# A diffusion-transformer step in fp32 on one core: where the second layer's modulation dots stand, and where three buffers of token sums lie

## The chip, the cores and the metric

The kernel runs on one core of one Trainium2 chip. A core has a matrix engine (TensorE, PE in the profile, its weight loads as PEld), a vector engine (VectorE, DVE), a scalar engine (ScalarE, ACT), GpSimd (POOL), a queue engine that issues transfers (SyncE, SP), and 16 DMA engines between main memory and the on-chip SBUF; matrix products land in PSUM. The metric is the device time of one execution in microseconds, the median of several runs.

## The reference, cut to what matters

Two layers act on 512 tokens of width 1024: 256 image tokens ("latent") and 256 context tokens. Each layer is a half feed-forward, a mixer (attention in layer 0, an mLSTM in layer 1), and a second half feed-forward. All of them are modulated by a vector per token group.

```python
def modulate(h, shift, scale):
    return h * (1.0 + scale) + shift

def half_ffn(h, shift, scale, gate, w_in, w_out, g, b):
    xm = modulate(h, shift, scale)
    a, u = jnp.split(xm @ w_in, 2, axis=-1)
    y = (jax.nn.silu(a) * u) @ w_out
    return post_norm(h, 0.5 * gate * y, g, b)
```

The hidden width is 2816, 22 blocks of 128. Shift, scale and gate are nine vectors of 1024 per layer, and each comes from the product of `silu(c)` with a 1024 x 9216 matrix `ada_w`, once for the latent tokens' vector `c` and once for the context tokens' vector. For layer 1 only the first feed-forward and the mixer's inputs need the context tokens' part, so the later chapters need one vector alone. Everything is fp32.

## The kernel before

**Products.** An fp32 product is made of three products in a reduced format: every operand is split into a high and a low part, and `mm3` issues high x high, high x low and low x high into the same PSUM tile (L234, by far the largest group of TensorE). Splitting (`split`) is a cast on ScalarE (L218) and a subtraction on VectorE (L223). Weights come as 512 KB tiles of 128 x 1024 over the SP queue (L203, a ring of three raw tiles), are split into a ring of seven pairs, and then feed TensorE.

**Feed-forwards.** Four run in this order with the mixers between: layer 0 first half, attention, layer 0 second half (here "block one", about 520 to 965 us), layer 1 first half ("block two", about 915 to 1330 us), mLSTM, and the last. In blocks one and two `ffn` does each feed-forward in two halves of 11 hidden blocks. In the first half, 11 units of 48 matmuls 512 wide make the hidden activations: `ffn_g` takes a silu on ScalarE (L558), a gate multiply on VectorE (L559) and a split. Four units form a "lead" whose calls for side work come together at the lead's end; each further unit j has one call behind it and two pieces of a residual (`residual`, VectorE at L533). Then eight output products of 33 matmuls 512 wide, one for each block of 128 output features, are added into the running state by VectorE (L679). In the second half the 11 units are done by `fast_in`: it computes the two-by-two block product of weights and tokens with seven instead of eight block products (a Strassen–Winograd scheme), 84 matmuls 256 wide in a unit. The products are issued in the order a11, a12, s1, s2, a22, s4, s3. Four of them (a11, a12, s1, s4) read the tokens as they are. s2, a22 and s3 read sums and differences of token blocks that are prepared once, by `fast_sums`: additions at L578, L582, L585, L587 and L590, each followed by a split. That preparation stands behind the fifth and sixth output product of the first half (d = 4 and 5, `SUMSAT = 4`). The second half then ends with its own output products: four 512 wide, and four in two halves 256 wide.

**The token sums' buffers.** `fast_operands` opens two buffers, `th` and `tl`, for the high and the low parts of three sums of 4 x 256 columns. They lie behind other buffers at bytes 196576 and 208864 of each partition, both 224 bytes past a multiple of 256, and so do all three sums within them. The tokens as they are lie at multiples of 256; the stationary weights lie 64 bytes past one.

**Modulation dots.** A tile of 128 outputs x 1024 inputs of `ada_w` is loaded by `ada_load` (L321, ring of two tiles named "ada", SP queue), and `ada_dot` (L327) multiplies it on VectorE with a vector that all partitions hold, with the sum accumulated: one instruction gives 128 outputs of one vector. The dots are pinned, that is, they keep their place in program order on VectorE. Layer 1 has 72 tiles; the first 40 get two dots (both vectors, a "pair"), the last 32 one dot (a "single"): 112 dots. `silu_c`, `silu_load` and `silu` make the vectors: two broadcast loads of 512 KB and two silu on ScalarE (L296). The buffers share room with those of `fast_in`, and so are closed and opened again. `emit` spreads the dots with hooks that `ffn` calls: behind each unit of the first half as many tiles as make four dots (`DOTS[0]`), behind each output product of the first half three (`DOTS[1]`), until the block's own list is empty. Block one's list has 28 pairs: 22 behind the units, six behind the first three output products. Block two's list has 12 pairs and 32 singles: the pairs and 20 singles behind the units, 12 singles behind the first four output products.

Of the kernel before, what the change touches and what calls it, by code (L numbers as in the profile page):

```python
# [86 lines left out]


SUMSAT = 4
DOTS = (4, 3)  # L90

TAILSTEP = {(0, 3, 1): 'bmccccccc', (1, 0, 2): 'c', (1, 0, 6): 'v', (1, 1, 7): 'rxxxxxxxx'}
MTAILSTEP = {(0, 7, 0): 'bmccccccc', (1, 0, 3): 'c', (1, 1, 0): 'v', (1, 6, 0): 'r', (1, 7, 2): 'xxxxxxxx'}
# [72 lines left out]
class Body:  # L166
# [123 lines left out]
    def silu_load(self, pin=lambda ins: ins):  # L290
        for v in range(2):
            pin(self.nc.sync.dma_start(self.cb[:, v, :], self.a["c2"][v : v + 1, :].broadcast_to([P, D])))

    def silu(self, pin=lambda ins: ins):
        for v in range(2):
# [265 lines left out]

    def fast_operands(self, st):

        self.th, self.tl = (self.t([P, 3, ND // 2, TL], F32R, pool=st) for _ in range(2))

    def fast_sums(self, i):

        V = self.nc.vector
        lo, up = slice(2 * i, 2 * i + 2), slice(ND // 2 + 2 * i, ND // 2 + 2 * i + 2)
        made = lambda k: (self.th[:, k, lo, :], self.tl[:, k, lo, :])  # L570

        def at(ks, g):
            return self.xh[:, ks, g[0] : g[1]], self.xl[:, ks, g[0] : g[1]]

        def whole(ks, g):
            o = self.tmp().rearrange("p (k f) -> p k f", k=2)
            h, l = at(ks, g)
            V.tensor_tensor(out=o, in0=h.bitcast(F32), in1=l.bitcast(F32), op=ALU.add)  # L578
# [12 lines left out]
        self.split(d, *made(2))  # L591

    def fast_in(self, j, w_in, st):

        nc, V, S = self.nc, self.nc.vector, self.nc.scalar
        half = 4 * P
        r0, r1 = (self.raw(w_in[2 * j + i]) for i in range(2))
        sums = self.t([P, 4 * half], tag="sums", bufs=1, pool=st)
        part = lambda x, i: x[:, i * half : (i + 1) * half]
        a11, a21, a12, a22 = part(r0, 0), part(r0, 1), part(r1, 0), part(r1, 1)  # L600
        s1, s2, s4, s3 = (part(sums, i) for i in range(4))
        add = lambda o, x, y: V.tensor_tensor(out=o, in0=x, in1=y, op=ALU.add)  # L602
# [12 lines left out]
        of = lambda k0, g: lambda k: self.x(k0 + k, g)  # L615
        made = lambda i: lambda k: (self.th[:, i, k, :], self.tl[:, i, k, :])

        def product(o, name, x, first, last):
            for k in range(ND // 2):
                c = slice(k * P, (k + 1) * P)  # L620
                self.mm3(o, [y[:, c] for y in w[name]], x(k), first and k == 0, last and k == ND // 2 - 1, group=False)

        x, yv, z = self.mm()[:, :TL], self.mm(), self.mm()[:, :TL]
        y, v = yv[:, :TL], yv[:, TL:]
        a, u = self.tmp(), self.tmp()
        product(x, "a11", of(0, LAT), True, False)
# [12 lines left out]
        u2 = u.rearrange("p (n f) -> p n f", n=2)  # L639
        V.scalar_tensor_tensor(u2, x[:, None, :].broadcast_to([P, 2, TL]), -1.0, u2, ALU.mult, ALU.subtract)  # L640
        V.tensor_tensor(out=a, in0=a, in1=u, op=ALU.mult)
        gh, gl = self.gt[j] = tuple(self.t([P, self.gw], F32R, tag=k, bufs=self.gn, pool=self.gp) for k in ("gh", "gl"))
        self.split(a, gh, gl)

    def ffn(self, layer, s, gate, groups, side, start=None, cpool=None):
# [4 lines left out]
        with self.tc.tile_pool(name=f"ffn{li}", bufs=1) as gp:  # L650
# [34 lines left out]
            for hf in range(2):  # L685
# [35 lines left out]
                body = ND - TAIL if hf else ND  # L721
                if fast:
                    more.close()
                for d in range(body):
                    if cpool and not hf and d == SUMSAT:
                        cpool.close()
                        self.n += 1
                        more = ExitStack()
                        st = more.enter_context(self.tc.tile_pool(name=f"st{self.n}", bufs=1, side="right"))
                        self.fast_operands(st)  # L730
                    unit_out(hf, d, w, allg)
                    if cpool and not hf and d >= SUMSAT and d - SUMSAT < 2:
                        self.fast_sums(d - SUMSAT)
                    call("out", hf, d)
                if body < ND:
                    w = Keep(self, w.chunks, SH, w)
                    self.fine = True
                    for g in groups:
                        for d in range(body, ND):
                            unit_out(hf, d, w, g, TAILSTEP)  # L740
                    self.steps('B')


    def ffn_last(self, layer, gate):
# [820 lines left out]
def emit(ctx, tc, a, out):  # L1565
    b = Body(ctx, tc, a, out)
    nc, V, S = b.nc, b.nc.vector, b.nc.scalar
    b.setup()
    b.setup_rest()
    cpool = b.silu_c()  # L1570
    both2 = (0, 1)
    queue = [
        [(0, p, both2) for p in range(16, 72)],
        [(1, p, both2) for p in range(28)],
        [(1, p, both2) for p in range(28, 40)] + [(1, p, (0,)) for p in range(40, 72)],
    ]
# [9 lines left out]
    def side(key, coef, keep=(True, True), nxt=True, ada=(), alone=False, fast=False):  # L1586
        def pop():
            for _ in range(3 if len(ada) > 40 else 2):
                if ada:
                    b.ada(*ada.pop(0))  # L1590

        def dots(n):
            while n > 0 and ada:
                n -= len(ada[0][2])
                b.ada(*ada.pop(0))

        get = once(key, coef)

        b.begin = lambda g: b.norm(g, get, keep[0 if g == LAT else 1], nxt, alone)
        s = {}  # L1600
        for j in range(NF):
            s["in", j] = (lambda: dots(DOTS[0])) if fast else pop
        for d in range(ND):
            s["out", 0, d] = (lambda: dots(DOTS[1])) if fast else pop
        return s

    both = (LAT, CTX)
    b.ffn(0, 0, once("g0", lambda: b.half_gate(0, 2)), both, side("n0", lambda: b.ln_mod(0, 0, (0, 3)), ada=queue[0]), start)
    assert not queue[0]
    cpool.close()  # L1610
    b.attention(lambda: b.shift_(0, 5), side("n1", lambda: b.ln_mod(0, 1, (0, 6))))
    cpool = b.silu_c()
    b.silu_load()
    b.silu()
    b.ffn(0, 1, once("g1", lambda: b.half_gate(0, 8)), both, side("n2", lambda: b.ln_mod(0, 2, (1, 0)), ada=queue[1], fast=True), cpool=cpool)
    assert not queue[1]
    cpool = b.silu_c()
    b.silu_load()
    b.silu()
    b.ffn(1, 0, once("g2", lambda: b.half_gate(1, 2)), both, side("n3", lambda: b.ln_mod(1, 0, (1, 3)), (True, False), ada=queue[2], fast=True), cpool=cpool)  # L1620
    assert not queue[2]
# [95 lines left out]
```

## Time and profile before

| | |
|---|---|
| runs | 1657.2, 1662.06, 1662.81 us (median 1662.06) |
| profiled execution | 1661.01 us, its span 1659.1 us |
| mean granted clock of TensorE | 0.992 |
| TensorE's matmuls busy | 1624.8 us, 98% of the span |
| VectorE busy | 1354.8 us, 82% |
| ScalarE busy | 743.6 us, 45% |

The span runs from the first to the last instruction that the profiler saw; the rest of the profiled execution's own time, 1.9 us, lies around it. Busy times are sums over an engine's instructions, and matmuls are pipelined, so a busy TensorE is not one at its peak. "PEclk", the granted clock, is the share of full speed that the throttle allowed. "Idle before" is the time an engine stood still ahead of an instruction, put down to the event that released it last. A time such as 1059.67 is counted from the span's start.

### The profile page before, as it was taken

The page shows a single profiled execution, that of the slowest core. Times are in us where ns is not written, and L with a number is a line of the kernel's source. Part 1 is how long each engine was busy: PE and PEld are TensorE (multiplying, and loading weights), DVE is VectorE, ACT ScalarE, POOL GpSimd, SP SyncE. Part 2 cuts the span into 40 slices and gives each one's busy share as a digit, 9 for nine tenths or more (in the row PEclk, how much of TensorE's full clock was granted, in tenths as well). Part 3 has the DMA queues.
Part 4 walks back from the last instruction along what each step waited for, and adds up shares of the span by engine and source line. Part 5 has one row for each costly group of instructions (what it writes and reads, how often), then busy time and mean ns, then how long its engine had stood idle before and what let it go on. Part 6 is the DMA issues. An engine that isn't in the chain of part 4 may idle for free. (4 is left out here: it accounts for less than half of the span.)

```text
span 1659.1 us, 26570 instructions
## 1 busy us (share of the span) xinstructions
PE 1624.8 (98%) x10308; PEld 1463.5 (88%) x10308; DVE 1354.8 (82%) x2689; ACT 743.6 (45%) x1267; POOL 62.3 (4%) x76
## 2 busy tenths in 40 slices
PE   9999999999989999999999999899999999999998
PEld 6888888899978998889999988689999989999987
DVE  5899977749898979999965888779975967897687
ACT  5532132314765443325652424215651566656542
POOL 0000000001010200000000100000000100020000
PEclk9999999999999999999999999898999999999999
DMA  9577766622203157733352267743351342438552
GB/s 372 188 234 234 246 203 193 200 64 84 64 1 113 54 158 223 218 113 117 113 179 69 84 203 251 256 126 103 127 153 55 111 134 78 128 115 253 179 178 89
DMA packets 72207, 251.54 MB, mean 152 GB/s; under 512 B 7952, under 2 KB 10768, under 8 KB 72080
## 3 DMA queue, kind: packets, MB, share of 16 engines
q1 hardware_dynamic: 71504, 249.05, 47.3%
q8 instruction: 81, 1.33, 0.3%
q10 hardware_dynamic: 576, 0.79, 0.1%
q14 instruction: 46, 0.38, 0.1%
HBM read 248.76 MB, written 1.05 MB: 151 GB/s over the span
## 5 line engine op out<-in xcount | busy, mean ns | idle before, releaser
L234 PE MATMUL t<-t,t 128*128 128x256 f32 (+2 forms) x8412 | 1332.6, 320 | 19.3 <-ACT t L218 15.1
L234 PEld LDWEIGHTS t<-t,t 128*128 128x128 f32 x8412 | 1199.4, 189 | 140.1 <-ACT t L218 17.6
L218 ACT CAST t<-t 128x1024 fp32r<-128x1024 f32 (+3 forms) x521 | 428.4, 843 | 481.7 <-PE t L234 233.4
L223 DVE TENSOR_TENSOR t<-t,t 128x256 fp32r<-128x256 f32 (+2 forms) x740 | 513.6, 728 | 116.9 <-ACT t L218 113.2
L327 DVE SCALAR_TENSOR_TENSOR t<-t,t 128x1024 bf16<-128x1024 f32 x224 | 263.8, 1221 | 28.2 <-DMA t<-in_ada_w 27.3
L894 PE MATMUL t<-t,t 128*128 128x256 f32 (+1 forms) x256 | 79.4, 310 | 0.0
L896 PE MATMUL t<-t,t 128*128 128x256 f32 (+1 forms) x256 | 78.7, 307 | 0.0
L895 PE MATMUL t<-t,t 128*128 128x256 f32 (+1 forms) x256 | 78.4, 306 | 0.0
L558 ACT ACTIVATE t<-t 128x512 f32<-128x512 f32 (+1 forms) x71 | 34.3, 488 | 95.4 <-PE t L234 95.3
L679 DVE SCALAR_TENSOR_TENSOR t<-t,t,t 128x256 f32<-128x256 f32 x96 | 42.6, 478 | 41.6 <-PE t L234 41.6
L559 DVE TENSOR_TENSOR t<-t,t 128x512 f32<-128x512 f32 (+1 forms) x71 | 38.9, 552 | 34.4 <-PE t L234 28.0
L454 POOL TENSOR_TENSOR t<-t,t 128x256 f32<-128x256 f32 x30 | 23.5, 785 | 1142.2 <-ACT t L444 1140.9
L1409 PE MATMUL t<-t,t 128*128 128x512 f32 (+3 forms) x286 | 60.2, 366 | 1.9 <-ACT t L1486 1.0
L822 PE MATMUL t<-t,t 128*128 128x512 f32 (+1 forms) x300 | 60.5, 364 | 0.0
L1409 PEld LDWEIGHTS t<-t,t 128*128 128x128 f32 (+2 forms) x286 | 43.8, 159 | 18.3 <-issue 2.3
L822 PEld LDWEIGHTS t<-t,t 128*128 128x128 f32 x300 | 51.5, 189 | 8.9
L444 ACT ACTIVATE t<-t 128x256 f32<-128x256 f32 x72 | 26.1, 411 | 72.0 <-DVE t L437 72.0
L534 ACT ACTIVATE t<-t,t 128x256 f32<-128x256 f32 x64 | 29.4, 503 | 56.6 <-DVE t L533 56.5
L894 PEld LDWEIGHTS t<-t,t 128*128 128x128 f32 x256 | 48.3, 189 | 2.6
L895 PEld LDWEIGHTS t<-t,t 128*128 128x128 f32 x256 | 48.2, 188 | 2.6
L896 PEld LDWEIGHTS t<-t,t 128*128 128x128 f32 x256 | 48.1, 188 | 2.5
L602 DVE TENSOR_TENSOR t<-t,t 128x512 f32<-128x512 f32 x66 | 45.3, 686 | 0.6
(200 smaller groups left out, 1066.3 us busy)
## 6 DMA issues: line engine op xcount, KB each, us to landing
t<-in_ffn_in SPq DMA_DIRECT2D x168, 512.0 KB, 4.0
t<-in_ada_w SPq DMA_DIRECT2D x137, 512.0 KB, 4.3
t<-in_ffn_out SPq DMA_DIRECT2D x66, 512.0 KB, 4.3
t<-in_ffn_last SPq DMA_DIRECT2D x22, 512.0 KB, 3.6
t<-in_att_in SPq DMA_DIRECT2D x12, 512.0 KB, 3.5
t<-in_att_out SPq DMA_DIRECT2D x8, 512.0 KB, 3.5
t<-in_ml_qk SPq DMA_DIRECT2D x8, 512.0 KB, 3.6
t<-in_ml_v SPq DMA_DIRECT2D x8, 512.0 KB, 3.6
```

The source lines that it names most:

```text
L218: self.behind(self.nc.scalar.copy(h, x))
L223: self.behind(self.nc.vector.tensor_tensor(out=ls, in0=xs, in1=hs.bitcast(F32), op=ALU.subtract))
L234: mm = lambda *k, **kw: self.nc.tensor.matmul(*k, skip_group_check=not group, **kw)
L327: ins = nc.vector.scalar_tensor_tensor(self.tmp().bitcast(BF16), r, 1.0, self.cb[:, v, :], ALU.mult, ALU.mult, accum_out=to)
L559: V.tensor_tensor(out=sl, in0=sl, in1=pu[:, :n], op=ALU.mult)
L602: add = lambda o, x, y: V.tensor_tensor(out=o, in0=x, in1=y, op=ALU.add)
L679: V.scalar_tensor_tensor(z, y[:, gg[0] - t0 : gg[1] - t0], gate()[:, v, d : d + 1], z, ALU.mult, ALU.add)
L822: pin(nc.tensor.matmul(o, gs[g], ws[k][w][:, i : i + n], start=k == k0 and g == w == 0, stop=k == k1 - 1 and g == 1,))
L894: mm(o, self.xh[:, k, c], wh, start=k == 0, stop=False)
L895: mm(o, self.xh[:, k, c], wl, start=False, stop=False)
L896: mm(o, self.xl[:, k, c], wh, start=False, stop=k == ND - 1)
L1409: mm = lambda *k, **kw: pin(nc.tensor.matmul(*k, **kw))
```

## The change

Three things are changed; all arithmetic stays.

1. The second layer's dots are one list, `later`, and each block takes its own numbers from it: block one four dots behind each unit, two pairs behind each of the first four output products of the first half, and one pair behind each of the four 512-wide output products of the second half (68 dots); block two three behind each unit (rounded up to whole pairs: six pairs, then 24 singles) and two singles behind each of the first four output products (44 dots). Its entry for the second half finds the list empty.
2. For the dots in the second half's output products the two vectors are loaded and their silu is taken there, inside `ffn` (`silu_all`), and the open buffers are handed to the next feed-forward. Block two does so too, and its vectors are not read again.
3. The three sums' high and low parts lie in one buffer, at byte 196352, a multiple of 256. Sum 0 and sum 1 (read by s2 and s3) follow one another at multiples of 256; sum 2 (read by a22) lies `FLIP` = 56 floats, that is 224 bytes, past one.

```diff
 SUMSAT = 4
-DOTS = (4, 3)
+FLIP = 56
+DOTS = {
+    1: {("in",): 4, ("out", 0): 3, ("out", 1): 2},
+    2: {("in",): 3, ("out", 0): 2, ("out", 1): 3},
+}
...
+    def silu_all(self):
+        pool = self.silu_c()
+        self.silu_load()
+        self.silu()
+        return pool
...
     def fast_operands(self, st):
 
-        self.th, self.tl = (self.t([P, 3, ND // 2, TL], F32R, pool=st) for _ in range(2))
+        n = ND // 2 * TL
+        x = self.t([P, 6 * n + FLIP], F32R, pool=st)
+        at = [2 * i * n + (FLIP if i == 2 else 0) for i in range(3)]
+        self.made = [[x[:, a + p * n : a + (p + 1) * n].rearrange("p (k f) -> p k f", f=TL) for p in range(2)] for a in at]
...
-        made = lambda k: (self.th[:, k, lo, :], self.tl[:, k, lo, :])
+        made = lambda k: [x[:, lo, :] for x in self.made[k]]
...
-        made = lambda i: lambda k: (self.th[:, i, k, :], self.tl[:, i, k, :])
+        made = lambda i: lambda k: [x[:, k, :] for x in self.made[i]]
...
                 if fast:
                     more.close()
+                    cpool = self.silu_all()
                 for d in range(body):
...
                     self.steps('B')
+        return cpool
...
-    queue = [
-        [(0, p, both2) for p in range(16, 72)],
-        [(1, p, both2) for p in range(28)],
-        [(1, p, both2) for p in range(28, 40)] + [(1, p, (0,)) for p in range(40, 72)],
-    ]
+    queue = [(0, p, both2) for p in range(16, 72)]
+    later = [(1, p, both2) for p in range(40)] + [(1, p, (0,)) for p in range(40, 72)]
...
-        def dots(n):
-            while n > 0 and ada:
-                n -= len(ada[0][2])
-                b.ada(*ada.pop(0))
+        def some(n):
+            while n > 0 and later:
+                n -= len(later[0][2])
+                b.ada(*later.pop(0))
...
         for j in range(NF):
-            s["in", j] = (lambda: dots(DOTS[0])) if fast else pop
+            s["in", j] = (lambda: some(dots["in",])) if dots else pop
         for d in range(ND):
-            s["out", 0, d] = (lambda: dots(DOTS[1])) if fast else pop
+            s["out", 0, d] = (lambda d=d: some(dots["out", 0] if d < SUMSAT else 0)) if dots else pop
+            s["out", 1, d] = lambda: some(dots.get(("out", 1), 0))
...
-    cpool = b.silu_c()
-    b.silu_load()
-    b.silu()
-    b.ffn(0, 1, once("g1", lambda: b.half_gate(0, 8)), both, side("n2", lambda: b.ln_mod(0, 2, (1, 0)), ada=queue[1], fast=True), cpool=cpool)
-    assert not queue[1]
-    cpool = b.silu_c()
-    b.silu_load()
-    b.silu()
-    b.ffn(1, 0, once("g2", lambda: b.half_gate(1, 2)), both, side("n3", lambda: b.ln_mod(1, 0, (1, 3)), (True, False), ada=queue[2], fast=True), cpool=cpool)
-    assert not queue[2]
+    cpool = b.silu_all()
+    cpool = b.ffn(0, 1, once("g1", lambda: b.half_gate(0, 8)), both, side("n2", lambda: b.ln_mod(0, 2, (1, 0)), dots=DOTS[1]), cpool=cpool)
+    cpool = b.ffn(1, 0, once("g2", lambda: b.half_gate(1, 2)), both, side("n3", lambda: b.ln_mod(1, 0, (1, 3)), (True, False), dots=DOTS[2]), cpool=cpool)
+    assert not later, len(later)
+    cpool.close()
```

More of the change, by code (lines that the diff above doesn't have):

```diff
@@ L1584, in once, with side @@
         return get
-    def side(key, coef, keep=(True, True), nxt=True, ada=(), alone=False, fast=False):
+    def side(key, coef, keep=(True, True), nxt=True, alone=False, dots={}):
         def pop():
-            for _ in range(3 if len(ada) > 40 else 2):
-                if ada:
-                    b.ada(*ada.pop(0))
-        def dots(n):
-            while n > 0 and ada:
-                n -= len(ada[0][2])
-                b.ada(*ada.pop(0))
+            for _ in range(3 if len(queue) > 40 else 2):
+                if queue:
+                    b.ada(*queue.pop(0))
+        def some(n):
+            while n > 0 and later:
+                n -= len(later[0][2])
+                b.ada(*later.pop(0))
         get = once(key, coef)
@@ L1601, in side @@
         for j in range(NF):
[L1602 removed]
+            s["in", j] = (lambda: some(dots["in",])) if dots else pop
         for d in range(ND):
[L1604 removed]
+            s["out", 0, d] = (lambda d=d: some(dots["out", 0] if d < SUMSAT else 0)) if dots else pop
+            s["out", 1, d] = lambda: some(dots.get(("out", 1), 0))
         return s
     both = (LAT, CTX)
[L1608 to L1609 removed]
+    b.ffn(0, 0, once("g0", lambda: b.half_gate(0, 2)), both, side("n0", lambda: b.ln_mod(0, 0, (0, 3))), start)
+    assert not queue
     cpool.close()
     b.attention(lambda: b.shift_(0, 5), side("n1", lambda: b.ln_mod(0, 1, (0, 6))))
[L1612 to L1621 removed]
+    cpool = b.silu_all()
[3 more added lines that the diff above has]
+    cpool.close()
     b.mlstm(lambda: b.shift_(1, 5, slice(0, 1)), side("n4", lambda: b.ln_mod(1, 1, (1, 6), 1), alone=True))
```

## The prediction

> **What bounds the kernel now.** I read the page first (busy time, costliest groups, DMA issues), then busy time in chosen stretches, then what TensorE and VectorE waited for in them, then their timelines.
>
> ```profile
> span 1659.1 us, 26570 instructions
> ...
> PE 1624.8 (98%) x10308; PEld 1463.5 (88%) x10308; DVE 1354.8 (82%) x2689; ACT 743.6 (45%) x1267; POOL 62.3 (4%) x76
> ...
> L327 DVE SCALAR_TENSOR_TENSOR t<-t,t 128x1024 bf16<-128x1024 f32 x224 | 263.8, 1221 | 28.2 <-DMA t<-in_ada_w 27.3
> ...
> t<-in_ada_w SPq DMA_DIRECT2D x137, 512.0 KB, 4.3
> ```
>
> TensorE is busy 98% of the span, so the time is the matmul stream plus what interrupts it or slows its clock: a gain must come from the 34 us in which PE is idle, or from a cheaper matmul. The dots (L327) are 264 us of VectorE, and nearly all idle time ahead of them is a wait for the modulation weights, whose tiles take 4.3 us to land. Next, stretches; the columns are length, then busy time and count of PE, weight load, VectorE, ScalarE, GpSimd, then granted clock, DMA share, GB/s. Each count includes about two matmuls that only touch an edge.
>
> ```profile
> 615.00:640.00 25.00, 25.00 (x112) 20.71 (x111) 22.67 (x36) 5.93 (x7) 0.00 (x0) 1.00 0.71 233
> 715.00:747.00 32.00, 32.00 (x143) 26.53 (x143) 31.64 (x55) 9.40 (x14) 0.00 (x0) 1.00 0.17 58
> 747.00:855.00 108.00, 108.00 (x922) 108.00 (x921) 95.36 (x124) 65.84 (x108) 0.00 (x0) 1.00 0.39 118
> ...
> 1015.00:1040.00 25.00, 25.00 (x112) 20.69 (x112) 20.56 (x40) 9.12 (x13) 0.00 (x0) 1.00 0.87 280
> ...
> 1051.00:1060.00 9.00, 0.80 (x4) 0.38 (x3) 6.43 (x11) 1.52 (x3) 0.00 (x0) 0.76 0.82 268
> 1060.00:1070.00 10.00, 10.00 (x33) 7.93 (x33) 7.13 (x12) 1.05 (x1) 0.00 (x0) 0.71 0.64 201
> 1070.00:1111.00 41.00, 41.00 (x183) 33.97 (x182) 30.52 (x60) 6.02 (x9) 0.00 (x0) 1.00 0.59 188
> ...
> 1117.00:1133.00 16.00, 11.83 (x66) 10.84 (x65) 13.35 (x23) 7.21 (x12) 0.00 (x0) 0.68 0.18 66
> ```
>
> Block one (rows up to 855) runs without a gap at 25.00/110 = 0.227 us per 512-wide matmul. Block two breaks twice. From 1051 to 1060 PE all but stops, and from 1060 to 1070 it does 31 matmuls at a clock of 0.71, worth 31 x 0.227 = 7.0 us: 8.2 + 3.0 = **11.2 us lost**. From 1117 to 1133 it does 64 matmuls 256 wide, at 108/920 = 0.1174 us worth 7.5 us of the 16: **8.5 us lost**. What they waited for (VectorE over 1000 to 1110, then over 640 to 720; TensorE over 1000 to 1140; total us, times, longest), and TensorE's timeline:
>
> ```profile
> DVE t L327 <- DMA t<-in_ada_w: 18.5, 21, 2.2
> ...
> DVE t L327 <- DMA t<-in_ada_w: 0.5, 1, 0.5
> ...
> PE t L234 <- ACT t L218: 12.0, 3, 8.2
> ...
> 1035.67 15.80 PE L234 MATMUL t<-t,t 128*128 128x512 f32 x69
> 1059.67 15.66 PE L234 MATMUL t<-t,t 128*128 128x512 f32 x55 [8.20 <-ACT t L218]
> 1119.85 0.39 PE L234 MATMUL t<-t,t 128*128 128x256 f32 x1 [1.55 <-ACT t L218]
> 1124.25 9.97 PE L234 MATMUL t<-t,t 128*128 128x256 f32 x56 [2.23 <-ACT t L218]
> ```
>
> The releaser is a cast, but ScalarE is idle; it has what VectorE gave it late:
>
> ```profile
> 990.11 1.23 DVE L327 SCALAR_TENSOR_TENSOR t<-t,t 128x1024 bf16<-128x1024 f32 x1 [1.17 <-DMA t<-in_ada_w]
> ...
> 1054.07 1.22 DVE L327 SCALAR_TENSOR_TENSOR t<-t,t 128x1024 bf16<-128x1024 f32 x1 [1.52 <-DMA t<-in_ada_w]
> 1056.35 1.23 DVE L327 SCALAR_TENSOR_TENSOR t<-t,t 128x1024 bf16<-128x1024 f32 x1 [1.04 <-DMA t<-in_ada_w]
> 1058.29 0.68 DVE L559 TENSOR_TENSOR t<-t,t 128x512 f32<-128x512 f32 x1
> ...
> 1098.48 1.23 DVE L327 SCALAR_TENSOR_TENSOR t<-t,t 128x1024 bf16<-128x1024 f32 x1 [1.38 <-DMA t<-in_ada_w]
> 1104.06 1.23 DVE L327 SCALAR_TENSOR_TENSOR t<-t,t 128x1024 bf16<-128x1024 f32 x1 [0.70 <-DMA t<-in_ada_w]
> 1105.21 1.89 DVE L578 TENSOR_TENSOR t<-t,t 128x512 f32<-128x512 f32 x3
> ...
> 717.75 1.89 DVE L578 TENSOR_TENSOR t<-t,t 128x512 f32<-128x512 f32 x3
> ...
> 1013.71 1.85 SPq L321 DMA_DIRECT2D t<-in_ada_w  x2
> 1055.33 2.60 SPq L321 DMA_DIRECT2D t<-in_ada_w  x2
> ```
>
> The chain of the first stop: a single (one dot per 512 KB tile, ring of two) repeats no faster than its tiles land. Eight such loads of two lie between the last two rows, so a single takes (1055.33 - 1013.71)/14 = 2.97 us; later, 1098.48 to 1104.06 over two, 2.79. Four are 11.2 to 11.9 us, and a unit (48 matmuls) is 10.9. The dots are pinned in program order on VectorE, so the last unit's gate multiply (L559) starts only at 1058.29. That unit's products ended at 1051.47 - 35 x 0.227 = 1043.5 (the 69 matmuls from 1035.67 include 30 of the output product that need no gate of unit 10, and 5 of the next). PE had work till then, and starts 1.38 us after L559.
>
> The second: the output products' singles hold back the token sums (L578) until 1105.2, 6 us before the 256-wide products that read them (from 1111). In block one they start at 717.75, 29 us before 747, and PE never waits.
>
> **Part one: the dots.** Twelve dots go from block two (56 to 44) to block one (56 to 68). In block two the first 12 dots are pairs, then 24 singles follow, three per call, and eight in the output products instead of 12. Three quantities decide.
>
> First stop. The first single stands where the 13th dot stood, at 990.1. Ahead of unit 10's gate multiply stand 21 singles (three at the lead's end, three behind each of units 4 to 9). With a period p, L559 starts at 990.1 + 20p + 2.0 (the last dot and the residual behind it, 1056.35 to 1058.29), and PE may go 1.4 us later. It has other work until 1043.5 + 30 x 0.227 = 1050.3. With p = 2.79 L559 is at 1047.9 and PE does not stop; with 2.97 it stops 2.6 us. I take 2.9, a stop of **1.2 us**, since three per unit ask for fewer bytes than the four in the row with DMA share 0.87. Gain 11.2 - 1.2 = 10.0.
>
> The clock is the open part. The row 1117 to 1133 shows 0.68 beside stops no longer than 2.23 us, so a stop of 1 to 3 us may cost as much again; I put that in the range. The Trainium skill's "TensorE: Matmul & The Clock Gate" (rules for sustained throughput) says that only idle gaps above about 3 us drop the clock: by it a 1.2 us stop costs itself alone, and three short stops cannot explain 0.68. The trace does not bear it out there.
>
> Second stop. After unit 10's gate 11 singles are left (three and eight): 11 x 2.9 = 32 us, to about 1082. The 256-wide products start eight times 33 x 0.227 = 60 us after 1044.7, about 1105: 23 us ahead, between the 29 that suffice and the 6 that do not, near the first. Gain **8.5**; bounds 0 and 8.5, near 8.5.
>
> Block one. Four more dots before its token sums (264/224 = 1.18 us each) and the rearranged order put them at about 725, still 22 us ahead of 747. The eight in the second half's four 512-wide output products are 9.4 us on VectorE, which was busy 95.36 of 108 us before, and in these 30 us is idle about half (14.81 of 30):
>
> ```profile
> 855.00:885.00 30.00, 30.00 (x135) 24.88 (x135) 14.81 (x39) 9.31 (x10) 0.00 (x0) 1.00 0.59 192
> 863.47 1.06 ACT L296 ACTIVATE t<-t 128x1024 f32<-128x1024 f32 x1 [4.89 <-DMA t<-in_c]
> ...
> 1242.89 1.05 ACT L218 CAST t<-t 128x1024 fp32r<-128x1024 f32 x1 [4.28 <-PE t L234]
> ```
>
> Queued behind a dot that waits for its tile are evacuations and weight splits; TensorE is then fed from PSUM buffers and weight pairs split ahead. On SP the tile loads stand between weight chunks and wait for a dot to free a buffer. The cover is that idle half: cost **0**. Uncovered, all 12 moved dots would cost 12 x 1.18 = 14 us, a single late token sum about 8.5.
>
> The vectors' loads and two Silu (L296, 1.06 us each) stay where they were in block one. In block two a third set appears that nothing reads: two Silu fit in ScalarE's 4.28 us waits for PE, two 512 KB loads in a stretch with no tiles. Cost **0**; uncovered, 2.1 us.
>
> **Part two: the addresses.** No instruction is added. In each of 22 units the products by sums 0 and 1 (24 matmuls) now read their moving operand at a multiple of 256 bytes, as direct ones do; only a22's 12 still sit 224 bytes past one. The last unit of block one, TensorE alone, cut at its products (36 direct, 24 by sums, 12 direct, 12 by a sum), then two long runs of direct ones elsewhere:
>
> ```profile
> 845.42:849.65 4.23, 4.23 (x38) 1.00 0.82 246
> 849.65:852.51 2.86, 2.86 (x26) 1.00 0.82 219
> 852.51:853.87 1.36, 1.36 (x14) 1.00 0.65 262
> 853.87:855.28 1.41, 1.41 (x14) 1.00 0.51 58
> 944.60:964.50 19.90, 19.90 (x172) 1.00 0.44 131
> 1569.70:1589.60 19.90, 19.90 (x178) 1.00 0.52 162
> ```
>
> Without the two edge matmuls: 117.5, 119.2, 113.3, 117.5 ns per matmul. So direct products run at 117.5 or 113.3, at full clock, and long runs show both (19.90/170 = 117.1; /176 = 113.1). Every run by sums turned the one into the other here. If the 12 left still turn it, two units together have as many at one rate as at the other, 36 and 36 on average: 4.23 + 4.08 + 1.41 = 9.72 us against 9.86, 22 x 0.14 = **-3.1 us**, my choice because it needs nothing but what the two runs in this unit did. If nothing turns it, all is slow (84 x 117.5 = 9.87, +0.2; with 119 for the 12 left, +0.6) or, without the slow state, 84 x 113.3 = 9.52, -7.5. These ends are in the range.
>
> The Trainium skill's "SBUF — State Buffer" (Who interferes with whom) speaks against this part: PE's moving operand and its weight load have independent ports, and PE never waits on anyone. By it addresses change nothing here. The trace has 113 and 118 ns for one shape, so something beyond shape counts, though not proven to be the address.
>
> **Sum**, against the profiled execution, 1661.0 us (span 1659.1 and 1.9 around it): 1661.0 - 10.0 - 8.5 - 3.1 + 0 = 1639.4. The three runs' median, 1662.06, is 1.05 higher; between both, I predict **1640 us**.
>
> **The rivals.**
> - Stops go, addresses bring nothing. For it: no row shows 24 aligned products in the place of these. 1640 + 3 = 1643 us. The skill's port rule would give this time.
> - Stops go, all products fast: 1640 - 4.4, about 1636. Against it: 944 to 964 ran 170 direct ones slowly.
> - The period is 3.1 us: the stop is 990.1 + 62 + 3.4 - 1050.3 = 5.2, and the clock falls as before (3.0): 1640 + 4.0 + 3.0 = 1647 us. For it: loads in block two now start beside different weight chunks.
> - Block one loses its cover: one late token sum there, as in the row 1117 to 1133, 8.5 us: 1648. Against it: 22 us of lead.
> - The change does not free VectorE: the pinned dots still hold the gate, 11.2 stays and only addresses or half of the second stop gain: about 1657.
> - **Slower**: the ring itself. Singles start 22 us earlier, and 21 rather than 16 stand ahead of the gate. First loss: 20p - 56.8, plus 3.0. It equals all that is gained (11.2 + 8.5 + 3.1 = 22.8) at p = 3.83; from there the kernel is slower. If the ring gave no overlap of landings, p = 4.3: 32.2 lost, 1661 + 9.4 = 1670. Against it: 2.97 at a DMA share of 0.87. For it: 4.3 is the page's own landing time.
>
> **How the numbers follow.** Forecast 0.46, addresses nothing 0.22, all fast 0.08, period 3.1 0.10, block one 0.05, not freed 0.04, slower 0.05. The range 1631 to 1652 holds the first five, with the bounds of the addresses and of p and the 3 us by which runs differ; it leaves out 0.09 and some edges. 0.3% (5 us) is about what a measurement of this kernel can tell from no change: faster 0.90, same 0.05 (not freed, and halves of its neighbours), slower 0.05.
>
> **What would show it.** No PE wait above 3 us around 1050 and granted clock 1.0 through block two; VectorE's 18.5 us of waits for the weights there more than halved; L559 of the last unit within 8 us of its products' end; token sums over 15 us ahead of their products; no PE wait from 640 to 885. For the addresses: 256-wide stretches of 22 units at 9.72 us each, alternating 113 and 118; 9.87 or 9.52 would show the other two. The forecast is wrong if a stop of several us is left at 1050, or if block one's PE waits.

## The result, and the profile after

The changed kernel takes 1651.92 us (median of 13 runs, 1648.66 to 1655.25) against 1660.81 us for the kernel before (13 runs): a ratio of 0.9948, 95% interval 0.9935 to 0.9960, 8.9 us faster. The forecast was 1640 us, some 21 us of gain. Its profiled execution took 1649.32 us (span 1647.6), 11.7 less than that of before; it is among the faster of its 13.

Line numbers have moved: matmuls are L238 (before L234), casts L222 (L218), splits L227 (L223), dots L337 (L327), tile loads L331 (L321), weight loads L207 (L203), the gate multiply L569 (L559), residuals L543 (L533). From the page of the changed kernel (span; the dots):

```profile
span 1647.6 us, 26587 instructions
...
L337 DVE SCALAR_TENSOR_TENSOR t<-t,t 128x1024 bf16<-128x1024 f32 x224 | 263.5, 1220 | 25.2 <-DMA t<-in_ada_w 24.5
```

The dots still wait 24.5 us for their tiles, where it was 27.3. Next, busy time in the stretches of block two (columns as before: length, busy time and count of PE, weight load, VectorE, ScalarE, GpSimd, then clock, DMA share, GB/s):

```profile
1040.00:1050.00 10.00, 9.76 (x44) 7.74 (x42) 6.32 (x11) 3.81 (x6) 0.00 (x0) 1.00 0.70 234
1050.00:1060.00 10.00, 2.69 (x6) 1.87 (x7) 6.95 (x12) 2.47 (x4) 0.00 (x0) 0.61 0.66 228
1060.00:1070.00 10.00, 10.00 (x41) 8.17 (x40) 8.28 (x15) 2.15 (x4) 0.00 (x0) 0.88 0.83 266
1070.00:1113.00 43.00, 43.00 (x192) 35.61 (x191) 38.82 (x72) 12.22 (x17) 0.00 (x0) 1.00 0.36 122
1113.00:1133.00 20.00, 20.00 (x174) 20.00 (x173) 18.50 (x28) 11.19 (x19) 0.00 (x0) 1.00 0.36 112
```

The second stop is gone: 1113 to 1133 runs at full clock without a gap. The first is there, and at 1050 to 1060 the clock falls again. What VectorE waited for over 1000 to 1110, TensorE over 1000 to 1140, and what TensorE did behind its wait:

```profile
DVE t L337 <- DMA t<-in_ada_w: 15.2, 15, 2.8
...
PE t L238 <- ACT t L222: 7.5, 1, 7.5
...
1057.31 55.96 PE L238 MATMUL t<-t,t 128*128 128x512 f32 x235 [7.55 <-ACT t L222]
```

A stop of 7.55 us stands where one of 8.20 stood. The 234 matmuls behind it, up to the first 256-wide one at 1112.98, take 55.7 us instead of 234 x 0.227 = 53.2: 2.5 us of clock. In all 10.0 us are lost there, against 11.2 before.

Why, VectorE's timeline and the SP queue's loads of the changed kernel show, over one unit (the last VectorE row is the start of the token sums):

```profile
1042.81 1.22 DVE L337 SCALAR_TENSOR_TENSOR t<-t,t 128x1024 bf16<-128x1024 f32 x1 [2.75 <-DMA t<-in_ada_w]
...
1043.96 0.87 DVE L543 SCALAR_TENSOR_TENSOR t<-t,t,t 128x256 f32<-128x256 f32 x2
1044.76 0.68 DVE L569 TENSOR_TENSOR t<-t,t 128x512 f32<-128x512 f32 x1
1046.37 1.83 DVE L227 TENSOR_TENSOR t<-t,t 128x1024 fp32r<-128x1024 f32 x2 [0.93 <-ACT t L222]
1048.11 1.22 DVE L337 SCALAR_TENSOR_TENSOR t<-t,t 128x1024 bf16<-128x1024 f32 x1
...
1049.25 1.22 DVE L337 SCALAR_TENSOR_TENSOR t<-t,t 128x1024 bf16<-128x1024 f32 x1
...
1050.40 1.22 DVE L227 TENSOR_TENSOR t<-t,t 128x1024 fp32r<-128x1024 f32 x1
1053.98 1.23 DVE L337 SCALAR_TENSOR_TENSOR t<-t,t 128x1024 bf16<-128x1024 f32 x1 [2.37 <-DMA t<-in_ada_w]
...
1055.93 0.68 DVE L569 TENSOR_TENSOR t<-t,t 128x512 f32<-128x512 f32 x1
...
1086.74 1.89 DVE L591 TENSOR_TENSOR t<-t,t 128x512 f32<-128x512 f32 x3
...
1044.07 0.33 SPq L331 DMA_DIRECT2D t<-in_ada_w  x1
1049.36 1.47 SPq L331 DMA_DIRECT2D t<-in_ada_w  x2
```

A unit's dots stand in a clump: two behind the gate multiply's splits, the third a little later. With two buffers the third dot's tile can be asked for only when the first dot has freed one. The first dot ends at 1049.3, the load goes out at 1049.36, and the third dot starts at 1053.98, 4.6 us on. That landing lies in series with the rest of VectorE's unit, from third dot to third dot: dot 1.15, residuals 0.80, gate multiply 0.60, a wait for the cast 1.0, splits 1.74, first dot 1.15, landing 4.7, together 11.2 = 1053.98 - 1042.81. A unit of TensorE is 10.9 us. So VectorE, late since the lead, hardly catches up, and the last gate multiply starts at 1055.93. The weight split ahead of the third dot runs from 1050.40 to 1051.6, while that dot's tile is still on its way, and lengthens nothing.

### The profile page after: what moved, and what is told of

Its sections match the earlier page's. It is cut to its first block, busy times and chain, and to the rows that moved or that the text cites. A ratio compares the mean times of both kernels' runs of the same rounds, so it can differ in the third digit from the quotient of the medians.

```text
span 1647.6 us, 26587 instructions
## 1 busy us (share of the span) xinstructions
PE 1617.8 (98%) x10308; PEld 1457.4 (88%) x10308; DVE 1353.8 (82%) x2689; ACT 744.2 (45%) x1269; POOL 61.6 (4%) x76
## 5 line engine op out<-in xcount | busy, mean ns | idle before, releaser
L238 PE MATMUL t<-t,t 128*128 128x256 f32 (+2 forms) x8412 | 1325.1, 319 | 14.2 <-ACT t L222 10.7
L238 PEld LDWEIGHTS t<-t,t 128*128 128x128 f32 x8412 | 1193.1, 189 | 133.9 <-ACT t L222 12.7
L222 ACT CAST t<-t 128x1024 fp32r<-128x1024 f32 (+3 forms) x521 | 429.6, 844 | 467.3 <-PE t L238 244.3
L227 DVE TENSOR_TENSOR t<-t,t 128x256 fp32r<-128x256 f32 (+2 forms) x740 | 514.7, 728 | 116.6 <-ACT t L222 112.5
L337 DVE SCALAR_TENSOR_TENSOR t<-t,t 128x1024 bf16<-128x1024 f32 x224 | 263.5, 1220 | 25.2 <-DMA t<-in_ada_w 24.5
L569 DVE TENSOR_TENSOR t<-t,t 128x512 f32<-128x512 f32 (+1 forms) x71 | 38.9, 551 | 32.8 <-PE t L238 26.7
```

The lines of the kernel that those rows point to most:

```text
L222: self.behind(self.nc.scalar.copy(h, x))
L227: self.behind(self.nc.vector.tensor_tensor(out=ls, in0=xs, in1=hs.bitcast(F32), op=ALU.subtract))
L238: mm = lambda *k, **kw: self.nc.tensor.matmul(*k, skip_group_check=not group, **kw)
L337: ins = nc.vector.scalar_tensor_tensor(self.tmp().bitcast(BF16), r, 1.0, self.cb[:, v, :], ALU.mult, ALU.mult, accum_out=to)
L569: V.tensor_tensor(out=sl, in0=sl, in1=pu[:, :n], op=ALU.mult)
```

## The experiments

Theory A: this loop through the ring of two. Theory B: the DMA engines cannot bring the tiles faster. Others are named where they come in. Times are medians, each beside runs of the kernel before on the same chip (1660.6 to 1660.9 us).

**A ring of three.** From block one's second half on:

```diff
-        r = self.t([P, 1024], tag="ada", bufs=2, pool=self.cp)
+        r = self.t([P, 1024], tag="ada", bufs=self.ring, pool=self.cp)
...
                     more.close()
+                    self.ring = 3
                     cpool = self.silu_all()
```

> The changed kernel with a ring of three modulation tiles instead of two, from block one's second half on. Theory A (the ring's own loop: within a unit the third dot's tile can be asked for only when the unit's first dot has freed its buffer, and its landing of 4.6 us then lies in series with the rest of VectorE's unit): the third tile is asked for a unit earlier, the last unit's gate multiply is on time, the PE stop of 7.5 us at 1050 and the clock fall behind it go, about 1642 us (10 below the changed kernel), and VectorE's 17 us of waits for modulation weights over 985 to 1110 fall below 6. Theory B (the tiles come as fast as the DMA engines can bring them beside the weight chunks): one more buffer brings no bytes sooner, the stop stays above 5 us, about 1652 us.

Measured 1641.28 us, ratio 0.9878 (0.9863 to 0.9892). VectorE's wait for tiles over 1000 to 1110 (first row), and busy time in two stretches:

```profile
DVE t L338 <- DMA t<-in_ada_w: 0.7, 1, 0.7
...
1040.00:1050.00 10.00, 10.00 (x46) 8.29 (x45) 7.00 (x11) 3.26 (x7) 0.00 (x0) 1.00 0.70 243
1050.00:1060.00 10.00, 10.00 (x46) 8.28 (x45) 8.34 (x22) 3.14 (x5) 0.00 (x0) 1.00 0.93 322
```

No stop, full clock, 15.2 us of waits down to 0.7. The engines carried 322 GB/s at 1050 to 1060 where the changed kernel had 228: theory B falls. The scheduler also placed the weight splits otherwise (no longer between the unit's dots), so the ring is not the only difference.

**The third dot without a tile of its own.** Behind block two's units the third dot reads the tile of the second; eight tiles and their dots' values are left out.

```diff
-        r = self.ada_load(layer, dt)
+        if not again:
+            self.last = self.ada_load(layer, dt)
...
+        r = self.last
```

> The changed kernel in which the third dot behind each unit of block two's first half loads no tile and reads the one of the dot before it, so eight tiles of the modulation weights are left out of the computation; the ring stays at two, and VectorE does as many dots as in the changed kernel. Theory A (the third dot's tile, asked for only when the unit's first dot is done, puts one landing in series with VectorE's unit): no dot waits for a tile asked for in its own unit, the stop at 1050 and the clock fall go, about 1642 us. Theory D (three dots and the splits are too much work for VectorE in a unit, or their order on VectorE is at fault, loads or not): the stop stays above 5 us, about 1652 us.

Measured 1640.74 us (0.9881, 0.9860 to 0.9903). VectorE's waits for tiles over 1000 to 1110:

```profile
DVE t L337 <- DMA t<-in_ada_w: 0.9, 2, 0.7
```

TensorE waited for nothing from 1000 to 1140. VectorE had as many dots as in the changed kernel, and the ring was two, so neither the dots' work nor the ring as such is the cause, but a third tile per unit in a ring of two. Here too the splits stand outside the dots' clump, so these two runs, which both take the third landing out of the loop, do not separate how far their place contributes. The ring of three in the kernel before, further down, does.

**Two per unit.**

```diff
-    2: {("in",): 3, ("out", 0): 2, ("out", 1): 3},
+    2: {("in",): 2, ("out", 0): 2, ("out", 1): 4},
```

> The changed kernel with block two's dots two behind each unit, two behind each of the first four output products of the first half, and the 14 that are left behind the four wide output products of its second half, whose vectors the changed kernel loads there anyway. Theories A and B both expect no stop at 1050: two dots per unit never wait for a tile asked for in the same unit, and bring fewer bytes; about 1642 us, no TensorE wait over 1 us between 985 and 1140. Theory C (not the dots but something else on VectorE or ScalarE makes the last unit's gate multiply late): a stop of 5 us or more stays there, about 1652 us. If the dots in the second half of block two lost their cover, TensorE would wait in 1200 to 1260: 1642 plus up to 14 x 1.2 = 17 us.

Measured 1649.85 us (ratio 0.9929, 0.9914 to 0.9944): a miss of 8 us. From 1000 to 1140 TensorE waited for nothing, as expected. It waited later (what it waited for over 1200 to 1300, its timeline, then VectorE's):

```profile
PE t L427 <- DVE t L404: 6.2, 1, 6.2
...
1259.69 1.22 PE L427 MATMUL t<-t,t 128*128 128x256 f32 x2 [6.19 <-DVE t L404]
...
1255.36 1.23 DVE L337 SCALAR_TENSOR_TENSOR t<-t,t 128x1024 bf16<-128x1024 f32 x1 [2.28 <-DMA t<-in_ada_w]
...
1258.08 0.42 DVE L404 TENSOR_TENSOR t<-t,t 128x256 f32<-128x256 f32 x1
```

Fourteen singles at the end of block two run through the same ring of two; pinned ahead of the normalisation's sums (L404), they hold them back 6 us, and the granted clock is 0.75 over the 10 us from 1260. The stop was moved, not removed. Theory C falls all the same, since nothing stops at 1050.

**The ring of three in the kernel before**, in block two alone:

```diff
     assert not queue[1]
+    b.ring = 3
     cpool = b.silu_c()
```

> The kernel before (dots 56 and 56, four and three per call, addresses as before) with a ring of three modulation tiles in block two alone. Theory A (the ring's loop makes both stops): a single can then follow every (4.3 + 1.2)/3 = 1.8 us, four per unit are 7.3 of 10.9 us, three per output product 5.5 of 7.5 us; both stops go, 19.7 us less than before, about 1641 us, without any dot moved. Theory B (too many bytes and dots for block two): with four per unit the DMA share stays near 0.87 and the stops stay above half, about 1652 us or more.

Measured 1642.96 us (0.9893, 0.9876 to 0.9910). VectorE's waits for tiles over 1000 to 1110, TensorE's over 1000 to 1140, one stretch, and a weight split and a dot of one unit:

```profile
DVE t L328 <- DMA t<-in_ada_w: 3.1, 5, 0.7
...
PE t L234 <- ACT t L631: 0.7, 1, 0.7
...
1040.00:1060.00 20.00, 20.00 (x90) 16.56 (x89) 17.74 (x30) 7.14 (x10) 0.00 (x0) 1.00 0.94 323
...
1043.49 1.23 DVE L223 TENSOR_TENSOR t<-t,t 128x1024 fp32r<-128x1024 f32 x1 [0.71 <-ACT t L218]
1045.34 1.23 DVE L328 SCALAR_TENSOR_TENSOR t<-t,t 128x1024 bf16<-128x1024 f32 x1 [0.62 <-DMA t<-in_ada_w]
```

Both stops go without a dot being moved: one buffer gives 17.7 us, twice what the change gives. In this trace a weight split still stands between a unit's third and fourth dot (the last two rows), and nothing stops: the place of the splits is not the cause.

**The eight dots taken out of block one's end again.**

```diff
-    1: {("in",): 4, ("out", 0): 3, ("out", 1): 2},
-    2: {("in",): 3, ("out", 0): 2, ("out", 1): 3},
+    1: {("in",): 4, ("out", 0): 3, ("out", 1): 0},
+    2: {("in",): 3, ("out", 0): 3, ("out", 1): 3},
```

> The changed kernel with the eight dots taken out of block one's second half again: block two then has three behind each unit (ten pairs, 18 singles), three behind each of the first four output products, and two behind the first wide output product of its second half. The stop at 1050: ten pairs instead of six stand ahead, so singles start later, 15 instead of 21 ahead of the last gate multiply, with the unit's loop of 10.9 us as before: a stop of 5 to 8 us stays. The second stop: 15 singles at 2.8 us behind the last gate bring the token sums about 10 us later than in the changed kernel, 13 to 16 us ahead of the products that read them, between the 26 that were enough and the 6 that cost 8.5 us: 0 to 4 us. In all 1652 to 1656 us. If the eight dots in block one cost time there (the cover not given), this kernel gets it back between 860 and 900 us.

Measured 1651.84 us (0.9946, 0.9931 to 0.9962), the same as the changed kernel. TensorE's waits from 1000 to 1140:

```profile
PE t L238 <- ACT t L222: 4.2, 2, 3.7
PE t L238 <- DVE t L227: 1.4, 2, 0.8
PE t L238 <- ACT t L645: 0.6, 1, 0.6
```

The first stop is shorter (3.7 us and 0.6 right behind it, less than the 5 to 8 expected). A part of the second is back: 1.8 us in three waits from 1113 to 1122, and waits of 0.2 us in several later units of block two, which then take 10.0 us instead of 9.745. The time is equal. So the eight dots at block one's end buy nothing in the time. Nor do they cost anything there.

**Each part alone.** The changed kernel with the old buffers (first), and the kernel before with the new one:

```diff
-        n = ND // 2 * TL
-        x = self.t([P, 6 * n + FLIP], F32R, pool=st)
...
+        th, tl = (self.t([P, 3, ND // 2, TL], F32R, pool=st) for _ in range(2))
+        self.made = [[th[:, i], tl[:, i]] for i in range(3)]
```

> The changed kernel with the token sums' buffers as before (all three sums 224 bytes past a multiple of 256). If the addresses gave what the forecast says, each of the 22 units goes back from 9.745 to 9.87 us: 2.75 us slower than the changed kernel, about 1654.7 us. If the addresses do not matter: units stay at 9.745 us, 1652 us.

> The kernel before with the new buffer of token sums alone (sums 0 and 1 at multiples of 256, sum 2 at 224 past one); the dots as before. If the two parts are independent: both stops stay, each unit 9.745 instead of 9.87 us, 2.75 us below the kernel before, about 1658 us. If the addresses do not matter: 1660.8 us.

Measured 1651.91 us for the dots alone (0.9941, 0.9926 to 0.9956) and 1657.32 for the addresses alone (0.9976, 0.9966 to 0.9986). The second gives 3.5 us, as expected within its interval. The first equals the changed kernel, where 2.75 more were expected; its four runs cover 1650.26 to 1652.63, and a difference of 2.75 is inside what the two intervals allow. In the profiles the clock hides a part of it: the changed kernel's has a fall of the clock at 460 us that this one has not (87 matmuls against 98 from 455 to 470, some 1.2 us). The traces are plainer on the units: 50 us of 256-wide products in each of the four kernels (length, PE busy and count, clock, DMA share, GB/s).

Before:

```profile
775.00:825.00 50.00, 50.00 (x428) 1.00 0.36 107
```

Changed, and with it two neighbouring units:

```profile
775.00:825.00 50.00, 50.00 (x433) 1.00 0.36 107
...
806.07:815.75 9.68, 9.68 (x87) 1.00 0.37 112
815.75:825.56 9.81, 9.81 (x87) 1.00 0.36 104
```

Dots alone, then addresses alone:

```profile
775.00:825.00 50.00, 50.00 (x429) 1.00 0.32 106
```

```profile
775.00:825.00 50.00, 50.00 (x434) 1.00 0.34 108
```

The new buffer brings four to six matmuls more in 50 us whatever the dots do: units alternate between 9.68 and 9.81 us, 9.745 on average, where the kernel before has 9.87 in each.

**All three sums aligned.** The buffer stays in its place, sum 2 follows without the 224 bytes:

```diff
-        at = [2 * i * n + (FLIP if i == 2 else 0) for i in range(3)]
+        at = [2 * i * n for i in range(3)]
```

> The changed kernel with all three sums at multiples of 256 (sum 2 too); the dots as changed. Theory T (the 256-wide stream has two lasting rates, 118 and 113 ns, and each run of matmuls whose moving operand lies off 256 bytes turns the one into the other; with none left nothing turns it): the seven products of a unit all run at the rate the stream enters with. Both blocks enter at 118, so 84 x 118 = 9.9 us per unit instead of 9.745, 3.4 us slower than the changed kernel, about 1655 us; if it entered fast, 9.52 us and about 1647 us. Theory U (an unaligned matmul is simply dearer, and the aligned ones recover behind it): 84 x 113.5 = 9.53 us per unit from the first unit on, 1647 us. The stop at 1050 stays under both.

Measured 1653.4 us (0.9955, 0.9938 to 0.9972). 50 us in block one, 50 in block two, and TensorE's waits at the start of block one's 256-wide products (740 to 775):

```profile
775.00:825.00 50.00, 50.00 (x443) 1.00 0.38 117
1130.00:1180.00 50.00, 50.00 (x427) 1.00 0.35 106
...
PE t L238 <- ACT t L643: 1.9, 2, 1.8
PE t L238 <- ACT t L640: 0.5, 1, 0.5
```

The time lies between the two cases because the blocks went different ways, and the 2.4 us of waits at the start of block one come on top. Same products, same addresses, same clock: block one runs nearly all of them at 113 ns, block two all of them at 118. So it is not that an unaligned matmul is merely dearer (theory U): the stream has two lasting rates. In block one it turned to the fast one in its first unit, at the first of TensorE's brief waits; in block two it entered slow, nothing turned it, and it stayed slow for 11 units.

**One turn on purpose.** Ring of three, all sums aligned, and three extra matmuls ahead of each block's first 256-wide unit, whose result is overwritten:

```diff
+        if j == NFH:
+            odd = [x[:, 0, FLIP : FLIP + TL] for x in (self.xh, self.xl)]
+            self.mm3(z, [y[:, :P] for y in w["a11"]], odd, True, True, group=False)
         product(x, "a11", of(0, LAT), True, False)
```

> The changed kernel with the ring of three, all three sums at multiples of 256, and, ahead of each block's first 256-wide unit, three extra matmuls 256 wide that read the tokens 224 bytes past a multiple of 256 into a PSUM tile that is overwritten. Theory T: these three turn the stream from 118 to 113 ns once, and nothing turns it back: units at 84 x 113.3 = 9.52 us against 9.745, 22 x 0.225 = 5 us less than the run with the ring of three alone, and 0.7 us for the extra matmuls: about 1637 us. If three matmuls do not turn it, units stay at 9.9 us, about 1645 us. Theory U: the same 1637 us.

Measured 1636.07 us (0.9853, 0.9835 to 0.9871). 50 us in block one and in block two:

```profile
775.00:825.00 50.00, 50.00 (x444) 1.00 0.36 117
1115.00:1165.00 50.00, 50.00 (x444) 1.00 0.36 106
```

Behind the three matmuls off 256 bytes the stream runs at 113 ns in both blocks: 9.52 us per unit, but for block one's first two, which take 9.79 and 9.87 us with brief gaps in them. No run has three aligned matmuls in that place, so that it is their address that turns the stream is taken from the units of the other runs and not shown here by itself.

**Two last versions.** The same with eight of block one's dots moved on to its end, and the ring (in block two alone), the alignment and the turn on the kernel before:

```diff
-    1: {("in",): 4, ("out", 0): 3, ("out", 1): 2},
+    1: {("in",): 4, ("out", 0): 2, ("out", 1): 4},
```

> The run with ring of three and one turn of the 256-wide stream, with eight of block one's dots moved on from the first half's output products (one pair instead of two behind each) to the second half's wide ones (two pairs instead of one): block one's token sums start some 4 us earlier, as in the kernel before. If the changed kernel's four extra dots there are what delays the weights of block one's first 256-wide unit (its units 0 and 1 took 9.88 and 10.01 us instead of 9.84 and 9.87 in the changed kernel's profile, up to 12.57 in that of the run with all sums aligned), that goes: 0.5 to 1.5 us less, about 1635 us, and no TensorE wait from 740 to 775. If sixteen dots at the end of block one are not hidden: 4.7 to 9 us more, 1641 to 1645 us, with TensorE waits from 860 to 910.

> The kernel before, its dots where they were, with the ring of three in block two, all three sums at multiples of 256 and the three extra matmuls that turn the stream once per block. Ring: 1643 us, as measured. One turn: 22 units at 9.52 instead of 9.87 us, 7.7 us less, and 0.7 for the extra matmuls: about 1636 us, as fast as the same two edits on the changed kernel (1636.07), so that moving the dots is worth nothing once the ring is three deep. If the moved dots are worth something of their own, this run is 2 us or more above.

Measured 1634.87 us (0.9848, 0.9833 to 0.9863) and 1638.26 us (0.9865, 0.9850 to 0.9880). In the first, block one's units 0 and 1 take 9.54 and 9.52 us, where the run it was made from (1636.07) has 9.79 and 9.87, and none of its 16 dots at block one's end shows. The two intervals overlap, so a gain of 1.2 us is not established. The second is 2.2 us above that run, which its expectation would read as moved dots having a worth of their own, but again the intervals overlap. Its trace has one stop left, at block two's first 256-wide unit. The token sums are done by then; VectorE is late with the weight sums behind them (L607), and the ScalarE copy that releases TensorE stands behind a cast that waits 2.76 us for one of those. That three singles per output product make it late is likely, not shown:

```profile
1106.39 7.77 PE L235 MATMUL t<-t,t 128*128 128x256 f32 x52 [2.37 <-ACT t L635]
```

The best version, 1634.87 us, is 26 us under the kernel before.

## Why the prediction was wrong

**The direction and what bounds the kernel: right.** The time came out of the two stops in block two and of the 256-wide rate.

**First stop: wrong, and it is nearly the whole miss** (8.8 of the 9.9 us between the forecast sum of 1639.4 and the profiled 1649.3). The step that failed is the period: "I take 2.9, a stop of 1.2 us, since three per unit ask for fewer bytes than the four". The 21 singles ahead of the last gate multiply run from 988.71 to 1053.98: a period of 65.27/20 = 3.26 us. The forecast's own formula gives with it 20 x 3.26 - 56.8 = 8.4 us, against 7.55 measured. So the place, the count and the way a stop follows were right; the period was taken from a stretch with four dots a unit, as if it were a property of the ring that fewer bytes can only shorten. The runs show that it isn't: how three dots in a clump meet two buffers puts one landing per unit in series, and the unit's loop of mostly 10.6 to 11.2 us (8.7 once) catches up on little in units of 10.9. The 2.97 was such a loop as well, divided by four. From the row below to the one at 1056.35, fourth dot to fourth dot in the kernel before, it is 12.0 us; within it the first dot ends at 1049.8, the third dot's load goes out at 1049.92, and that dot starts at 1054.07. Three dots instead of four take about one dot's 1.15 us out of that loop, not a quarter of it.

```profile
1044.39 1.23 DVE L327 SCALAR_TENSOR_TENSOR t<-t,t 128x1024 bf16<-128x1024 f32 x1 [1.04 <-DMA t<-in_ada_w]
```

The rival with a period of 3.1 had the price nearly right (5.2 and 3.0 us against the 10.0 measured), but its reason (other weight chunks alongside) does not hold: bytes were not scarce.

**Second stop: right.** Predicted 8.5 gained; no wait is left from 1060 to 1140, and the token sums start at 1086.7, 26 us ahead, where 23 was forecast. That it is the fewer singles behind the output products which did it is supported by the run that puts 15 there: 1.8 us of waits came back.

**Addresses: right in mechanism, 0.5 us short.** Units alternate as forecast; 22 x (9.865 - 9.745) = 2.6 us against 3.1. The Trainium skill's "SBUF — State Buffer" (Who interferes with whom), by which PE waits on no one, gave no reason for the units to change; the run with all sums aligned, with 443 and 427 matmuls in 50 us at the same addresses and one clock, shows that PE's rate has another condition.

**Block one: nearly right.** The eight dots at its end cost nothing in any trace. The four extra ones ahead of its token sums do: the sums start at 724.5 as forecast (725), but units 0 and 1 take 9.88 and 10.01 us instead of 9.745, with a wait of 0.2 us; other profiles of kernels with the changed dots there have waits of 0.3 to 2.4 us in that place (ring of three with one turn: none listed, but units of 9.79 and 9.87 instead of 9.52 us), those of kernels with the old dots none. "Cost 0" was 0.4 us in this profile.

**The sum.** -1.2 - 8.5 - 2.6 + 0.4 = -11.9 us; the profiled executions differ by 11.7. The medians differ by 8.9. The 2.8 in between are not settled: the profiled execution is a fast one of its kernel, and the uneven waits in block one's first units and falls of the clock that only some executions have (last section) are candidates, not shown.

**The clock.** A stop of 1.2 us was to cost itself alone, or as much again. The changed kernel does not test it, since its stop stayed long; two experiments do (last section): stops of 1.6 and 1.8 us cost no clock. But the clock fell behind shorter ones elsewhere, so neither of the two prices holds in general.

## What to carry to other kernels

A load ring's period is not the landing time divided by its depth: where n consumers stand in a clump in an in-order queue and the ring is shallower than n, one whole landing can fall in series with everything else in that queue, as it did here, and the loop is then counted per clump and not per tile. Before work is spread out to relieve such a queue, try one buffer more: here it was worth 17.7 us by itself, and the whole change 8.9. And work that waits for loads, if it is pinned, can take its stop along: 14 dots moved to block two's end held TensorE up 6.2 us there, though eight at block one's end cost nothing.

## What the runs showed of the hardware

The stream of 256-wide matmuls has two lasting rates, 113 and 118 ns, at full granted clock and with equal shapes. With all moving operands at multiples of 256 bytes and no wait of TensorE neither rate changes over 11 units. A run of matmuls whose moving operand lies 224 bytes past such a multiple turns the one into the other, in both directions; behind three of them, ahead of a block, the stream was fast each time. A brief wait of TensorE turned it too: with all sums aligned, block one's first unit ran at 118 ns ahead of its waits and at 113 behind them (34 and 78 matmuls without the two at the edges):

```profile
748.45:752.45 4.00, 4.00 (x36) 1.00 0.76 250
758.95:767.75 8.80, 8.80 (x80) 1.00 0.31 113
```

Whether every wait does is not shown, and what the two states are is open.

The granted clock can fall behind short stops of TensorE. Behind the one of 2.37 us (the kernel before with ring and one turn; length, PE busy and count, clock, DMA share, GB/s) it was 0.67 for 5 us, and 24 matmuls took 213 ns instead of 113:

```profile
1106.40:1111.50 5.10, 5.10 (x30) 0.67 0.60 206
1111.50:1116.00 4.50, 4.50 (x42) 1.00 0.66 185
```

Behind one of 1.78 us (all sums aligned) and one of 1.63 (third dot without a tile), block one's first unit in both, it stayed at 1.00:

```profile
758.17:763.00 4.83, 4.83 (x42) 1.00 0.40 165
```

```profile
757.00:762.00 5.00, 5.00 (x47) 1.00 0.36 112
```

But the length of a stop does not decide alone. Ahead of block one, in work that no edit touches, TensorE waits 0.7 and 1.2 us shortly before 462 us in all thirteen profiles; the clock from 455 to 470 is 0.89 in nine of them and 1.00 in four. The kernel before, then dots alone:

```profile
455.00:470.00 15.00, 13.16 (x87) 0.89 0.00 1
```

```profile
455.00:470.00 15.00, 13.16 (x98) 1.00 0.00 1
```

So no limit in the length of a stop follows from these runs, and what else decides is not shown. The Trainium skill's "TensorE: Matmul & The Clock Gate" (Why this matters for your kernels) asks for no idle gaps above about 3 us; in these runs the clock fell behind shorter ones.
